# Strassen FFN on one Trainium2 core: the last phase's tile arithmetic on VectorE, and S3·T3 ahead of S4·B22

## The chip, the cores and the metric

One core of one Trainium2 chip runs the whole program in one launch. The metric is the device time of one execution in microseconds. The profile shows TensorE (PE, with its weight loads as PEld), VectorE (DVE), ScalarE (ACT), GpSimd (POOL) and the queue of SyncE (SP), which issues most of the DMAs.

## The reference, cut to what matters

The program is two transformer-like blocks in a row; the change touches only the last part of the second, its feed-forward network:

```
h = rms_norm_2(x, pre2_w) * (1 + sc2) + sh2
gate, up = split(h @ ffn_w_in, 2)           # 1024 tokens x 1024 -> 2 x 2816
y = (silu(gate) * up) @ ffn_w_out           # 1024 x 2816 -> 1024 x 1024
x = x + (1 + gt2) * rms_norm_2(y, post2_w)
```

Everything is fp32.

## The kernel before, in words

Activations lie with their features on the 128 partitions and the 1024 tokens along the free axis, in halves of H = 512. Each fp32 operand is split into a high part, which ACT copies (`hi`, `ah`, `tv`), and a low part, which DVE forms as source minus high (`lo`, `al`, `tv`). `mm3` multiplies such a pair by three matmuls (high·high, high·low, low·high). So every operand tile costs one ACT copy and one DVE subtraction before PE can use it.

The last phase, `phase_f`, does the following in order.

- The out projection, and `mid(0)` and `mid(1)` beside it: norm, residual, second norm, and the activation operands of the first FFN product, in two token halves. `mid(1)` makes T1, T2, B22, T3 and T4 in this order, four tiles of 128x512 each. T3 and T4 are differences of tiles `res`, by `psub`.
- The first FFN product (L1825 `variant`, L2091 `rest`). It is done as one level of Strassen-Winograd in 11 groups of the hidden dimension, with the weight variants A0, A1, S1, S2, S4, S3 and A22 in each group. Per group the variant code forms S1 (`padd`), S2, S4 and S3 (`psub`) for two weight blocks, eight operations of 128x512. Groups 0 to 3 first do A0 and A1, then the rest. The results go to DRAM as `ffa` (DMAs on POOL's queue).
- The second FFN product (the loop from L2277), 8 products n = 0 to 7 in the order of the tables `WV` and `XV`: A11·B11, S1·T1, S2·T2, S4·B22, S3·T3, A12·B21, and A22·T4 in two halves of 256 tokens. Each runs over KH = 11 blocks k with four PSUM banks. `fetch` loads activation tiles `c` from `ffa`, 7 steps of k ahead of the matmuls, into 8 buffers (SP queue). `parts` forms T1, T2, T3 and T4 by `psub` and splits them, 5 steps ahead, into 6 buffers `ah` and `al`. `variant2` loads weight blocks (`quad`, 128x2x512, from `wfo`, also on SP's queue) and forms S1, S2 and S4 in the tiles `sc`, and S3 from two fresh loads. `drain` adds a product's four PSUM banks into the output sums `yu`, `yz`, `yw`, `yx`.
- `finish`: norm of the result, residual, output. The token sums go over PE (transposes, L2480), so they stand in PE's order. Half of the residual additions are on POOL (L2230) except in the last piece.

`psub` and `padd` (L1859, L1856) are GpSimd's `tensor_tensor`; `psplit` is the split with its subtraction on GpSimd. It is used for T4 in the second product and for four variants of group 0. `add`, `sub` and `tt` (L2439) and `stt` (L2451) are DVE's; `act` (L2465) is ACT's.

PE's instructions run in the order in which the program writes them. For the other engines and the DMA queues a scheduler fixes the order when the program is built, from its own idea of when each operand will be there. Every engine then runs its instructions strictly in that fixed order. Generators such as `mid`, `drain` and `finish` are advanced by `tick` while the matmuls are written, which places their transposes in PE's order.

Of the kernel before, what the change touches and what calls it, by code (L numbers as in the profile page):

```python
# [8 lines left out]
F32 = mybir.dt.float32  # L9
F32R = mybir.dt.float32r  # L10
U32 = mybir.dt.uint32
AF = mybir.ActivationFunctionType
ALU = mybir.AluOpType
# [3 lines left out]
P = 128  # L17
T = 1024
H = 512
# [1745 lines left out]
class PhaseF:  # L1765

    WV = ["A11", "S1", "S2", "S4", "S3", "A12", "A22", "A22"]
    XV = [("B11", 0, H), ("T1", 0, H), ("T2", 0, H), ("B22", 0, H), ("T3", 0, H), ("B21", 0, H), ("T4", 0, 256), ("T4", 256, H)]  # L1770
    KH = 11


# [49 lines left out]
    def variant(self, n, g, v):  # L1823

        if n == 0:  # L1825
            self.fetch_raws(-1)
        hi = self.ring.tile([P, 1024], F32R, tag="hi", name=self.name("hi"))
        lo = self.ring.tile([P, 1024], F32R, tag="lo", name=self.name("lo"))
        if v[0] == "A" and len(v) == 2:
            self.split(hi, lo, self.raws["g", 2 * g + int(v[1])])  # L1830
        else:
            if v == "S1":
                self.sl[g] = self.base.tile([P, T], F32, tag="rmask", name=self.name("sl"))
            for i in range(2):
                c = slice(i * H, i * H + H)
                j = 2 * g + i
                up, s = self.raws["u", j], self.sl[g][:, c]
                gate = self.raws.get(("g", j))
                if v == "S1":
                    self.padd(s, up[:, :H], up[:, H:])  # L1840
                elif v == "S2":
                    self.psub(s, s, gate[:, :H])
                elif v == "S4":
                    self.psub(s, gate[:, H:], s)
                elif v == "S3":
                    s = self.fl.tile([P, H], F32, tag="s3", name=self.name("s3"), bufs=1)
                    self.psub(s, gate[:, :H], up[:, :H])
                else:
                    s = up[:, H:]
                (self.psplit if g < 1 and v != "A22" else self.split)(hi[:, c], lo[:, c], s)  # L1850
        self.fetch_raws(n)
        return hi, lo


    def padd(self, out, a, b):
        self.nc.gpsimd.tensor_tensor(out=out, in0=a, in1=b, op=ALU.add)  # L1856

    def psub(self, out, a, b):
        self.nc.gpsimd.tensor_tensor(out=out, in0=a, in1=b, op=ALU.subtract)  # L1859

    def psplit(self, hi, lo, src):

        self.act(hi, src, AF.Copy)
        self.psub(lo, src, hi.bitcast(F32))

    def quad(self, i, j, e, tag=None):

# [8 lines left out]
    def variant2(self, v, e):  # L1876
        n = (2 if e < 5 else 1) * H
        if v == "S1":
            s = self.sc[e] = self.sp.tile([P, n], F32, tag=f"sc{e}", name=f"sc{e}")
            a, b = self.quad(1, 0, e), self.quad(1, 1, e, "ru")  # L1880
            self.add(s, a, b)
        elif v in ("S2", "S4"):
            s, a = self.sc[e], self.quad(0, v == "S4", e)
            if v == "S2":
                self.sub(s, s, a)
            else:
                self.sub(s, a, s)
        elif v == "S3":
            s, b = self.quad(0, 0, e), self.quad(1, 0, e, "ru")
            self.sub(s, s, b)  # L1890
        else:
            s = self.quad(int(v[1]) - 1, int(v[2]) - 1, e)
        hi = self.ring.tile([P, 1024], F32R, tag="hi", name=self.name("hi"))
        lo = self.ring.tile([P, 1024], F32R, tag="lo", name=self.name("lo"))
        self.split(hi[:, :n], lo[:, :n], s)
        return hi, lo

    def phase_f(self, x):
        nc, tc = self.nc, self.tc
# [15 lines left out]
        y = self.resid()  # L1915
# [23 lines left out]
        def mid(half):  # L1939
# [74 lines left out]
                yield from wait(2)  # L2014
            for k in range(4):
                t = y[k][:, hs]
                self.psub(t, y[k + 4][:, hs], t)
                tags = (("acc0", "acc1"), ("acc0b", "acc1b"), ("rb0", "rb1"))
                self.split(*put("T3", *(tile2(tags[k]) if k < 3 else tile1(0))), t)
                yield from wait(2)  # L2020
            for k in range(4):
                t = y[k + 4][:, h0]
                self.psub(t, y[k][:, h0], t)
                self.split(*put("T4", *tile1(1 + k)), t)
                yield from wait(2)

# [95 lines left out]
        items = [(n, k) for n in range(8) for k in range(self.KH)]  # L2122
        made, fetched, tch = {}, {}, {}
        cnt = [0, 0]
        FETCH, AHEAD = 7, 5

        def fetch(upto):
            while cnt[0] < min(upto, len(items)):
                n, k = items[cnt[0]]
                cnt[0] += 1  # L2130
                v, t0, t1 = self.XV[n]
                k1, k2 = k, k + self.KH
                src = {"B11": [(k1, 0)], "B21": [(k2, 0)], "T1": [(k1, H), (k1, 0)], "T2": [(k2, H)], "B22": [(k2, H)],
                       "T3": [(k2, H), (k1, H)], "T4": []}[v]
                fetched[n, k] = ts = []
                for row, o in src:
                    ts.append(fl.tile([P, H], F32, tag="c", name=self.name("c"), bufs=8)[:, : t1 - t0])
                    nc.sync.dma_start(ts[-1], self.ad[row][:, o + t0 : o + t1])

        def parts(upto, dst=None):  # L2140
            while cnt[1] < min(upto, len(items)):
                n, k = items[cnt[1]]
                cnt[1] += 1
                v, t0, t1 = self.XV[n]
                f = fetched.pop((n, k))
                t = f[0] if f else tch[k][:, t0:t1]
                if v == "T1":
                    t = tch[k] = self.sp.tile([P, H], F32, name=f"tch{k}")
                    self.psub(t, f[0], f[1])
                elif v == "T2":  # L2150
                    t = tch[k]
                    self.psub(t, f[0], t)
                elif v == "T3":
                    self.psub(t, f[0], f[1])
                elif v == "B21":
                    self.psub(tch[k], tch[k], t)
                d = dst
                if d is None:
                    d = [self.sp.tile([P, H], F32R, tag=q, name=self.name(q), bufs=AHEAD + 1)[:, : t1 - t0] for q in ("ah", "al")]
                made[n, k] = d  # L2160
                (self.psplit if v == "T4" else self.split)(*d, t)

        def early_parts():
            fetch(3)
            t = [fl.tile([P, T], F32R, tag="ru", name=self.name("ae"), bufs=2) for _ in range(2)]
            t.append(self.hpool.tile([P, T], F32R, tag="h6", name=self.name("ae")))
            for k in range(3):
                parts(k + 1, (t[k][:, :H], t[k][:, H:]))

        for g in range(self.LEAD):  # L2170
# [24 lines left out]
        yv = {}  # L2195
# [12 lines left out]
        def finish(t0, t1):  # L2208
            n = t1 - t0
            half, o = t0 // H, t0 % H  # L2210
            hr = slice(t0 // P, t1 // P)
            rb = tp.tile([P, H], F32, tag="rb", name=self.name("rb"))[:, :n]
            xs = []
            for m in range(8):
                if m % 2 == 0:
                    t = tp.tile([P, 1024], F32, tag=f"sc{m // 2}", name=self.name("X"))
                xs.append(t[:, m % 2 * H : m % 2 * H + n])
                nc.sync.dma_start(xs[m], self.x3d[m][:, t0:t1])
            tail = t1 == H
            if not tail:  # L2220
                yield
            if t1 == 256:
                yield
            r = []
            yield from self.rstd_rows(accs[half][:, o : o + n], rt[:, hr], rtmp[:, hr], None if tail else rb, 1, r)
            rb = r[0] if tail else rb
            for m in range(8):
                t = yv[m, half][:, o : o + n]
                self.stt(t, t, c3[:, m : m + 1], rb, ALU.mult, ALU.mult)
                (nc.gpsimd if t1 < T and m % 2 else nc.vector).tensor_tensor(out=t, in0=t, in1=xs[m], op=ALU.add)  # L2230
                nc.sync.dma_start(self.out[m][:, t0:t1], t)
                if t1 == T and m % 2:
                    yield

        def drain(n, pss):

            for m, ps in enumerate(pss):
# [13 lines left out]
                    self.add(u, ps, u)  # L2251
                    self.add(w, ps, w)
                elif n == 3:
                    x = yv[m, 1] = tp.tile([P, H], F32, name=f"yx{m}")
                    self.add(x, ps, yv[m + 4, 1])
                    square(1, x)
                elif n == 4:
                    w = yv[m + 4, 1]
                    self.add(w, ps, w)
                    square(1, w)  # L2260
                    self.add(u, ps, u)
                elif n == 5:
                    self.add(z, ps, z)
                    square(0, z)
# [329 lines left out]
```

## Time and profile before

| | |
|---|---|
| runs, device time | 2215.13, 2215.93, 2217.55 us; median 2215.93 |
| the profiled execution, own time | 2213.25 us |
| its span (first to last instruction of the core) | 2211.4 us |
| PE busy | 2138.3 us, 97% of the span |
| DVE busy | 1511.8 us, 68% |
| ACT busy | 900.2 us, 41% |
| POOL busy | 394.7 us, 18% |

Times in the rows below count from the span's start. The profiled execution's own time is 1.85 us longer than its span, and 2.68 us below the median of the runs. The out projection ends and the first FFN product starts at about 1500 us; the second product begins at 1952 us, and its last matmul ends at 2194 us. A row of a timeline gives the start, the length of one instruction or of several of one kind in a row, and in brackets the idle time before it with the instruction that ended it.

### The profile page before, as it was taken

The page shows a single profiled execution, that of the slowest core. Times are in us where ns is not written, and L with a number is a line of the kernel's source. Part 1 is how long each engine was busy: PE and PEld are TensorE (multiplying, and loading weights), DVE is VectorE, ACT ScalarE, POOL GpSimd, SP SyncE. Part 2 cuts the span into 40 slices and gives each one's busy share as a digit, 9 for nine tenths or more (in the row PEclk, how much of TensorE's full clock was granted, in tenths as well). Part 3 has the DMA queues.
Part 4 walks back from the last instruction along what each step waited for, and adds up shares of the span by engine and source line. Part 5 has one row for each costly group of instructions (what it writes and reads, how often), then busy time and mean ns, then how long its engine had stood idle before and what let it go on. Part 6 is the DMA issues. An engine that isn't in the chain of part 4 may idle for free.

```text
span 2211.4 us, 29459 instructions
## 1 busy us (share of the span) xinstructions
PE 2138.3 (97%) x10998; PEld 1766.7 (80%) x10998; DVE 1511.8 (68%) x2160; ACT 900.2 (41%) x1522; POOL 394.7 (18%) x388
## 2 busy tenths in 40 slices
PE   8999999999999999999999999999799999999896
PEld 7988888887898898787887778877588888887676
DVE  7675687676595533759665347769958767669697
ACT  5553553443255553434262122445423323334243
POOL 1000000001111200000000000013644434325245
PEclk9999999999999999999999999999899999999998
DMA  5011106320553343265565176644143222377744
GB/s 176 30 41 45 47 29 214 100 86 29 188 170 110 109 135 129 94 202 180 159 205 162 69 241 190 210 162 136 60 138 115 86 86 72 108 249 251 243 164 160
DMA packets 149815, 297.59 MB, mean 135 GB/s; under 512 B 21520, under 2 KB 43936, under 8 KB 149416
## 3 DMA queue, kind: packets, MB, share of 16 engines
q1 hardware_dynamic: 135128, 271.33, 37.9%
q0 software_dynamic: 8128, 20.07, 2.6%
q10 hardware_dynamic: 6416, 4.31, 0.7%
q8 instruction: 87, 1.43, 0.3%
q14 instruction: 56, 0.46, 0.1%
HBM read 232.55 MB, written 61.90 MB: 133 GB/s over the span
## 4 chain that ended last, share of the span: by engine, by line
PE 73%; DVE 11%; issue 6%; DMA 5%; ACT 3%; POOL 2%; SPq 0%; POOLq 0%; DVEq 0%; ACTq 0%
PE mm L2471 55%; PE sm L2471 17%; DVE lo L2439 2%; DVE al L2439 2%; PE sm L2480 1%; DVE sc L2439 1%; POOL res L1859 1%; ACT hi L2465 1%; DVE acc L2439 1%; DMA ru<-in_wfi 1%; DVE rl L2451 1%; DMA adar<-in_adaw 1%; DMA mD<-mlrows 1%; DVE B L2451 0%; POOL lo L1859 0%
## 5 line engine op out<-in xcount | busy, mean ns | idle before, releaser
L2471 PE MATMUL mm<-rh,hi 128*128 128x512 f32 x1552 | 623.5, 402 | 0.6 <-DVE c L2439 0.4
L2471 PE MATMUL mm<-rh,lo 128*128 128x512 f32 x1552 | 605.7, 390 | 0.0
L2471 PE MATMUL mm<-rl,hi 128*128 128x512 f32 x1552 | 605.1, 390 | 0.2 <-DVE rl L2439 0.2
L2471 PEld LDWEIGHTS mm<-rh,hi 128*128 128x128 f32 x1552 | 291.4, 188 | 70.6 <-issue 9.1
L2471 PEld LDWEIGHTS mm<-rh,lo 128*128 128x128 f32 x1552 | 291.4, 188 | 62.5
L2471 PEld LDWEIGHTS mm<-rl,hi 128*128 128x128 f32 x1552 | 291.9, 188 | 59.8 <-issue 3.1
L2465 ACT ACTIVATE hi<-raw 128x1024 fp32r<-128x1024 f32 (+2 forms) x189 | 182.6, 970 | 363.9 <-PE mm L2471 265.1
L2439 DVE TENSOR_TENSOR lo<-raw,hi 128x1024 fp32r<-128x1024 f32 (+2 forms) x189 | 221.1, 1173 | 107.0 <-ACT hi L2465 105.4
L2471 PE MATMUL mm<-yr,hi 128*128 128x512 f32 x384 | 119.2, 390 | 1.3 <-ACT yr L2465 0.8
L2471 PE MATMUL mm<-tv,hi 128*128 128x512 f32 x312 | 102.0, 407 | 14.5 <-DVE tv L2439 7.1
L2471 PE MATMUL mm<-hi,rh 128*128 128x256 f32 (+1 forms) x384 | 110.7, 288 | 0.0
L2471 PE MATMUL mm<-hi,rl 128*128 128x256 f32 (+1 forms) x384 | 109.2, 284 | 0.0
L2471 PE MATMUL mm<-lo,rh 128*128 128x256 f32 (+1 forms) x384 | 109.2, 284 | 0.0
L1856 POOL TENSOR_TENSOR sl<-ru 128x512 f32<-128x512 f32 x22 | 37.9, 1722 | 307.3 <-DMA ru<-in_wfi 307.3
L2451 DVE SCALAR_TENSOR_TENSOR adaa<-adar,cact,adaa 128x512 f32<-128x512 f32 x84 | 62.9, 749 | 37.0 <-DMA adar<-in_adaw 36.1
L2471 PEld LDWEIGHTS mm<-yr,hi 128*128 128x128 f32 x384 | 72.1, 188 | 17.7 <-DVE yr L2451 1.6
L2471 PEld LDWEIGHTS mm<-tv,hi 128*128 128x128 f32 x312 | 60.8, 196 | 31.4 <-DVE tv L2439 9.4
L2465 ACT ACTIVATE hi<-sl 128x512 fp32r<-128x512 f32 x66 | 39.3, 626 | 110.1 <-PE sm L2471 64.1
L2554 POOL TENSOR_TENSOR hss<-hss,mhalf 128x4 f32<-128x4 f32 x16 | 16.2, 1015 | 361.8 <-DVE hss L2457 361.8
L2471 PEld LDWEIGHTS mm<-hi,rh 128*128 128x128 f32 x384 | 73.4, 191 | 1.7 <-issue 1.2
L2471 PE MATMUL mm<-yr,lo 128*128 128x512 f32 x192 | 74.7, 389 | 0.0
L2471 PEld LDWEIGHTS mm<-hi,rl 128*128 128x128 f32 x384 | 73.4, 191 | 0.7 <-issue 0.2
(526 smaller groups left out, 4255.3 us busy)
## 6 DMA issues: line engine op xcount, KB each, us to landing
raw<-in_w SPq DMA_DIRECT2D x60, 512.0 KB
adar<-in_adaw SPq DMA_DIRECT2D x96, 256.0 KB
c<-ffa SPq DMA_DIRECT2D x88, 256.0 KB
raw<-in_wfo SPq DMA_DIRECT2D x40, 512.0 KB
raw<-in_wfi SPq DMA_DIRECT2D x30, 512.0 KB
raw<-in_wo SPq DMA_DIRECT2D x24, 512.0 KB
ru<-in_wfi SPq DMA_DIRECT2D x22, 512.0 KB
raw<-in_wpj SPq DMA_DIRECT2D x32, 256.0 KB
```

Source lines behind the costliest of these rows:

```text
L1856: self.nc.gpsimd.tensor_tensor(out=out, in0=a, in1=b, op=ALU.add)
L1859: self.nc.gpsimd.tensor_tensor(out=out, in0=a, in1=b, op=ALU.subtract)
L2439: self.nc.vector.tensor_tensor(out=out, in0=a, in1=b, op=op)
L2451: self.nc.vector.scalar_tensor_tensor(out=out, in0=a, scalar=s, in1=b, op0=op0, op1=op1)
L2465: self.nc.scalar.activation(out=out, in_=a, func=f, scale=scale, **kw)
L2471: self.nc.tensor.matmul(out, lhsT=l, rhs=r, start=start, stop=stop)
L2480: self.nc.tensor.transpose(out, a, self.ident[:n, :n])
L2554: self.nc.gpsimd.tensor_tensor(out=out, in0=tmp, in1=self.mhalf[:, : out.shape[1]], op=ALU.pow)
```

## The change

All `tensor_tensor` work of this phase on tiles moves from GpSimd to VectorE: `padd`, `psub` and `psplit` are gone, and `add`, `sub` and `split` stand in their place. The residual additions of `finish` are all VectorE's. In the second product S3·T3 becomes product n = 3 and S4·B22 n = 4. S3 is formed as A22 − S2 (one load) in place of A11 − A21 (two loads), and T3 as T2 − B11 (one reload of B11) in place of B22 − B12 (two loads). For k of 7 and above B11 is loaded straight into the tile `tch`, stays there, and is not loaded again for T1. `drain` follows the new order.

```diff
-    WV = ["A11", "S1", "S2", "S4", "S3", "A12", "A22", "A22"]
+    WV = ["A11", "S1", "S2", "S3", "S4", "A12", "A22", "A22"]
...
                 if v == "S1":
-                    self.padd(s, up[:, :H], up[:, H:])
+                    self.add(s, up[:, :H], up[:, H:])
                 elif v == "S2":
-                    self.psub(s, s, gate[:, :H])
+                    self.sub(s, s, gate[:, :H])
...
-                (self.psplit if g < 1 and v != "A22" else self.split)(hi[:, c], lo[:, c], s)
+                self.split(hi[:, c], lo[:, c], s)
...
         elif v == "S3":
-            s, b = self.quad(0, 0, e), self.quad(1, 0, e, "ru")
-            self.sub(s, s, b)
+            s = self.quad(1, 1, e)
+            self.sub(s, s, self.sc[e])
...
             for k in range(4):
                 t = y[k][:, hs]
-                self.psub(t, y[k + 4][:, hs], t)
+                self.sub(t, y[k + 4][:, hs], t)
...
-                src = {"B11": [(k1, 0)], "B21": [(k2, 0)], "T1": [(k1, H), (k1, 0)], "T2": [(k2, H)], "B22": [(k2, H)],
-                       "T3": [(k2, H), (k1, H)], "T4": []}[v]
+                src = {"B11": [(k1, 0)], "B21": [(k2, 0)], "T1": [(k1, H)] + [(k1, 0)] * (k < FETCH), "T2": [(k2, H)],
+                       "T3": [(k1, 0)], "B22": [(k2, H)], "T4": []}[v]
...
                 if v == "T1":
-                    t = tch[k] = self.sp.tile([P, H], F32, name=f"tch{k}")
-                    self.psub(t, f[0], f[1])
+                    if k < FETCH:
+                        tch[k] = self.sp.tile([P, H], F32, name=f"tch{k}")
+                    t = tch[k]
+                    self.sub(t, f[0], f[1] if k < FETCH else t)
...
                 elif v == "T3":
-                    self.psub(t, f[0], f[1])
+                    self.sub(t, tch[k], t)
...
-                (self.psplit if v == "T4" else self.split)(*d, t)
+                self.split(*d, t)
...
                 elif n == 3:
-                    x = yv[m, 1] = tp.tile([P, H], F32, name=f"yx{m}")
-                    self.add(x, ps, yv[m + 4, 1])
+                    w = yv[m, 1] = yv[m + 4, 1]
+                    x = yv[m + 4, 1] = tp.tile([P, H], F32, name=f"yx{m}")
+                    self.add(x, ps, w)
+                    self.add(u, ps, u)
                     square(1, x)
                 elif n == 4:
-                    w = yv[m + 4, 1]
+                    w = yv[m, 1]
                     self.add(w, ps, w)
                     square(1, w)
-                    self.add(u, ps, u)
```

As built, POOL has 208 rows in place of 384, DVE 2279 in place of 2100, SP's queue 805 in place of 826 (loads of `c` from `ffa` 69 in place of 88, straight into `tch` 4 in place of none, loads of `ru` from `wfo` 6 in place of 12).

Three places show how the order moves. The first is DVE's order around the making of T3 and T4 in `mid(1)`, up to the first addition (`w<-mm_13679`) that frees a PSUM bank of the first product's S1 and S2. Before, behind the split of B22 (`rl`):

```order
L2439 TENSOR_TENSOR rl_12780<-res_12444,rh_12772 128x512
L2439 TENSOR_TENSOR tv_13733<-res_12440,tv_13732 128x512
L2439 TENSOR_TENSOR tv_13744<-res_12441,tv_13743 128x512
...
L2439 TENSOR_TENSOR tv_13791<-res_12444,tv_13791 128x512
L2439 TENSOR_TENSOR lo_13773<-sl_13774,hi_13772 128x512
L2439 TENSOR_TENSOR tv_13801<-res_12445,tv_13801 128x512
L2439 TENSOR_TENSOR tv_13816<-res_12446,tv_13816 128x512
L2439 TENSOR_TENSOR w_13723<-mm_13679,c_13214 128x512
```

and in the change:

```order
L2437 TENSOR_TENSOR rl_12780<-res_12444,rh_12772 128x512
L2437 TENSOR_TENSOR res_12440<-res_12444,res_12440 128x512
L2437 TENSOR_TENSOR res_12441<-res_12445,res_12441 128x512
...
L2437 TENSOR_TENSOR sl_13774<-ru_13719 128x512
L2437 TENSOR_TENSOR tv_13759<-res_12442,tv_13758 128x512
L2437 TENSOR_TENSOR sl_13774<-ru_13721 128x512
...
L2437 TENSOR_TENSOR res_12444<-res_12440,res_12444 128x512
...
L2437 TENSOR_TENSOR res_12447<-res_12443,res_12447 128x512
L2437 TENSOR_TENSOR w_13723<-mm_13679,c_13214 128x512
```

The subtractions that form T3 and T4 (`res<-res,res`) and the next variant (`sl<-ru`) now stand in DVE's own line, ahead of `w`.

The second place is DVE's order at the start of the second product, where `al_16546` is the low part of B11 for k = 3. Before:

```order
L2439 TENSOR_TENSOR lo_16519<-raw_16516,hi_16518 128x1024
L2439 TENSOR_TENSOR al_16546<-c_16537,ah_16545 128x512
```

and in the change:

```order
L2437 TENSOR_TENSOR lo_16519<-raw_16516,hi_16518 128x1024
L2437 TENSOR_TENSOR tch_16703<-c_16649,c_16651 128x512
L2437 TENSOR_TENSOR tch_16735<-c_16679,c_16681 128x512
L2437 TENSOR_TENSOR al_16546<-c_16537,ah_16545 128x512
```

T1's subtractions for k = 0 and 1, which belong to the next product, now stand ahead of it, and the four loads of `c` that they read stand on SP's queue ahead of the loads of B11 for k = 7 to 10.

The third place is SP's queue where S3's weights are loaded. Before, in the product S4·B22 (`c_17488<-ffa_13184` is the second operand of T3 for k = 0):

```order
L1873 DMA raw_17607<-in_wfo 128x2x512
L1873 DMA ru_17609<-in_wfo 128x2x512
L2138 DMA c_17466<-ffa_13205 128x512
L2138 DMA c_17486<-ffa_13195 128x512
L1873 DMA ru_17639<-in_wfo 128x2x512
L1873 DMA ru_17697<-in_wfo 128x2x512
L2218 DMA X_18061<-x3d_12454 128x512
L2138 DMA c_17488<-ffa_13184 128x512
L2218 DMA X_18061<-x3d_12455 128x512
L2218 DMA X_18064<-x3d_12456 128x512
L2138 DMA c_17515<-ffa_13196 128x512
L2138 DMA c_17517<-ffa_13185 128x512
```

and in the change, at the end of S2·T2:

```order
L1863 DMA raw_17192<-in_wfo 128x2x512
L2133 DMA c_17199<-ffa_13205 128x512
L2133 DMA c_17220<-ffa_13184 128x512
L1863 DMA raw_17239<-in_wfo 128x2x512
L2133 DMA c_17246<-ffa_13185 128x512
L2133 DMA c_17265<-ffa_13186 128x512
L1863 DMA raw_17284<-in_wfo 128x2x512
L2133 DMA c_17291<-ffa_13187 128x512
```

Each weight block of S3 is now one load with two activation loads behind it, no `ru` and no `X` between.

## Rows read from the trace of the kernel before

**Rows 1.** The page's busy times in us; the number behind x counts instructions.

```profile
PE 2138.3 (97%) x10998; PEld 1766.7 (80%) x10998; DVE 1511.8 (68%) x2160; ACT 900.2 (41%) x1522; POOL 394.7 (18%) x388
```

**Rows 2.** PE's waits from 1300 us on: total us, times, longest.

```profile
PE mm L2471 <- DVE al L2439: 12.5, 5, 8.7
PE mm L2480 <- DVE acc L2439: 10.8, 3, 4.6
PE mm L2471 <- DVE tv L2439: 7.1, 3, 3.6
PE mm L2471 <- DVE w L2439: 4.0, 1, 4.0
```

**Rows 3.** Windows: us, then PE, PEld, DVE, ACT, POOL busy, PEclk, DMA share, GB/s.

```profile
1541.00:1592.00 51.00, 35.81 (x117) 25.73 (x118) 49.10 (x50) 24.49 (x42) 35.65 (x21) 0.78 0.21 67
1610.00:1950.00 340.00, 339.59 (x1497) 280.40 (x1496) 241.12 (x316) 100.85 (x158) 133.43 (x109) 1.00 0.30 100
1952.00:1982.00 30.00, 30.00 (x134) 24.86 (x133) 18.74 (x19) 11.03 (x17) 9.87 (x7) 1.00 0.91 306
1982.00:2012.70 30.70, 30.33 (x134) 24.52 (x133) 28.36 (x21) 13.56 (x23) 21.02 (x12) 1.00 0.77 262
2012.70:2047.30 34.60, 31.29 (x134) 24.43 (x133) 33.53 (x34) 15.46 (x22) 10.03 (x5) 1.00 0.77 260
...
2078.20:2120.90 42.70, 33.25 (x134) 26.60 (x133) 31.15 (x29) 15.73 (x24) 23.18 (x15) 0.88 0.65 213
2120.90:2159.00 38.10, 34.32 (x140) 27.66 (x139) 34.80 (x42) 13.49 (x22) 13.39 (x10) 0.91 0.44 152
...
2174.90:2194.10 19.20, 16.76 (x138) 16.39 (x136) 15.57 (x26) 7.49 (x16) 12.98 (x14) 1.00 0.27 90
```

**Rows 4.** Timelines of DVE and POOL in `mid(1)`.

```profile
1544.12 2.44 DVE L2451 SCALAR_TENSOR_TENSOR res<-res,c,rb 128x512 f32<-128x512 f32 x2 [1.04 <-ACT rb L2465]
1562.85 1.75 DVE L2439 TENSOR_TENSOR tv<-res,tv 128x512 fp32r<-128x512 f32 x1
1589.61 0.68 DVE L2439 TENSOR_TENSOR w<-mm,c 128x512 f32<-128x512 f32 x1
...
1560.67 8.43 POOL L1859 TENSOR_TENSOR res<-res,res 128x512 f32<-128x512 f32 x5 [0.63 <-DVE res L2439]
```

**Rows 5.** Timeline of DVE at the start of the second product, POOL idle.

```profile
1954.81 3.09 DVE L2439 TENSOR_TENSOR al<-c,ah 128x512 fp32r<-128x512 f32 x5
```

**Rows 6.** Group by form, DVE, 1610 to 1950 us: busy, mean ns, idle before.

```profile
L2451 DVE SCALAR_TENSOR_TENSOR c<-c,c 128x512 f32<-128x512 f32 x18 | 22.9, 1271 | 0.3
```

**Rows 7.** Timelines at n = 0: SP, ACT, PE, POOL.

```profile
1953.79 0.34 SPq L2138 DMA_DIRECT2D c<-ffa  x1
1958.02 0.32 SPq L2138 DMA_DIRECT2D c<-ffa  x1
1960.78 1.08 SPq L2138 DMA_DIRECT2D c<-ffa  x1
...
1957.42 0.64 ACT L2465 ACTIVATE ah<-c 128x512 fp32r<-128x512 f32 x1 [1.64 <-DMA c<-ffa]
...
1960.53 0.39 PE L2471 MATMUL mm<-al,hi 128*128 128x512 f32 x1
...
1969.32 1.35 POOL L1859 TENSOR_TENSOR tch<-c,c 128x512 f32<-128x512 f32 x1 [14.72 <-DMA c<-ffa]
```

**Rows 8.** Timelines at n = 4: SP, DVE.

```profile
2075.87 8.60 SPq L2138 DMA_DIRECT2D c<-ffa  x5
2084.53 0.43 SPq L1873 DMA_DIRECT2D raw<-in_wfo  x1
...
2088.76 1.23 DVE L2439 TENSOR_TENSOR raw<-raw,ru 128x1024 f32<-128x1024 f32 x1 [14.96 <-issue]
```

**Rows 9.** Timeline of PE at n = 5.

```profile
2140.63 1.12 PE L2480 MATMUL mm<-ident,acc 128*128 128x128 f32 x4 [3.78 <-DVE acc L2439]
```

**Rows 10.** POOL's waits, 1952 to 2160 us.

```profile
POOL tch L1859 <- DMA c<-ffa: 37.6, 14, 14.7
```

More of the change, by code (lines that the diff above doesn't have):

```diff
@@ L1765 @@
 class PhaseF:
-    WV = ["A11", "S1", "S2", "S4", "S3", "A12", "A22", "A22"]
-    XV = [("B11", 0, H), ("T1", 0, H), ("T2", 0, H), ("B22", 0, H), ("T3", 0, H), ("B21", 0, H), ("T4", 0, 256), ("T4", 256, H)]
+    WV = ["A11", "S1", "S2", "S3", "S4", "A12", "A22", "A22"]
+    XV = [("B11", 0, H), ("T1", 0, H), ("T2", 0, H), ("T3", 0, H), ("B22", 0, H), ("B21", 0, H), ("T4", 0, 256), ("T4", 256, H)]
     KH = 11
@@ L1839, in variant @@
                 if v == "S1":
-                    self.padd(s, up[:, :H], up[:, H:])
+                    self.add(s, up[:, :H], up[:, H:])
                 elif v == "S2":
-                    self.psub(s, s, gate[:, :H])
+                    self.sub(s, s, gate[:, :H])
                 elif v == "S4":
-                    self.psub(s, gate[:, H:], s)
+                    self.sub(s, gate[:, H:], s)
                 elif v == "S3":
                     s = self.fl.tile([P, H], F32, tag="s3", name=self.name("s3"), bufs=1)
-                    self.psub(s, gate[:, :H], up[:, :H])
+                    self.sub(s, gate[:, :H], up[:, :H])
                 else:
                     s = up[:, H:]
-                (self.psplit if g < 1 and v != "A22" else self.split)(hi[:, c], lo[:, c], s)
+                self.split(hi[:, c], lo[:, c], s)
         self.fetch_raws(n)
         return hi, lo
[L1855 to L1864, printed above, removed]
     def quad(self, i, j, e, tag=None):
@@ L2022, in mid @@
                 t = y[k + 4][:, h0]
-                self.psub(t, y[k][:, h0], t)
+                self.sub(t, y[k][:, h0], t)
                 self.split(*put("T4", *tile1(1 + k)), t)
@@ L2124, in phase_f @@
         cnt = [0, 0]
-        FETCH, AHEAD = 7, 5
+        FETCH, AHEAD, EARLY = 7, 5, 3
         def fetch(upto):
@@ L2132, in fetch @@
                 k1, k2 = k, k + self.KH
-                src = {"B11": [(k1, 0)], "B21": [(k2, 0)], "T1": [(k1, H), (k1, 0)], "T2": [(k2, H)], "B22": [(k2, H)],
-                       "T3": [(k2, H), (k1, H)], "T4": []}[v]
+                src = {"B11": [(k1, 0)], "B21": [(k2, 0)], "T1": [(k1, H)] + [(k1, 0)] * (k < FETCH), "T2": [(k2, H)],
+                       "T3": [(k1, 0)], "B22": [(k2, H)], "T4": []}[v]
                 fetched[n, k] = ts = []
                 for row, o in src:
-                    ts.append(fl.tile([P, H], F32, tag="c", name=self.name("c"), bufs=8)[:, : t1 - t0])
+                    if v == "B11" and k >= FETCH:
+                        ts.append(self.sp.tile([P, H], F32, name=f"tch{k}"))
+                        tch[k] = ts[-1]
+                    else:
+                        ts.append(fl.tile([P, H], F32, tag="c", name=self.name("c"), bufs=8)[:, : t1 - t0])
                     nc.sync.dma_start(ts[-1], self.ad[row][:, o + t0 : o + t1])
@@ L2147, in parts @@
                 if v == "T1":
-                    t = tch[k] = self.sp.tile([P, H], F32, name=f"tch{k}")
-                    self.psub(t, f[0], f[1])
+                    if k < FETCH:
+                        tch[k] = self.sp.tile([P, H], F32, name=f"tch{k}")
+                    t = tch[k]
+                    self.sub(t, f[0], f[1] if k < FETCH else t)
                 elif v == "T2":
                     t = tch[k]
-                    self.psub(t, f[0], t)
+                    self.sub(t, f[0], t)
                 elif v == "T3":
-                    self.psub(t, f[0], f[1])
+                    self.sub(t, tch[k], t)
                 elif v == "B21":
-                    self.psub(tch[k], tch[k], t)
+                    self.sub(tch[k], tch[k], t)
                 d = dst
@@ L2160, in parts @@
                 made[n, k] = d
-                (self.psplit if v == "T4" else self.split)(*d, t)
+                self.split(*d, t)
         def early_parts():
-            fetch(3)
+            fetch(EARLY)
             t = [fl.tile([P, T], F32R, tag="ru", name=self.name("ae"), bufs=2) for _ in range(2)]
             t.append(self.hpool.tile([P, T], F32R, tag="h6", name=self.name("ae")))
-            for k in range(3):
+            for k in range(EARLY):
                 parts(k + 1, (t[k][:, :H], t[k][:, H:]))
@@ L2229, in finish @@
                 self.stt(t, t, c3[:, m : m + 1], rb, ALU.mult, ALU.mult)
-                (nc.gpsimd if t1 < T and m % 2 else nc.vector).tensor_tensor(out=t, in0=t, in1=xs[m], op=ALU.add)
+                self.add(t, t, xs[m])
                 nc.sync.dma_start(self.out[m][:, t0:t1], t)
```

## The prediction

> **What bounds the kernel now.** I read the page's busy times first: PE is busy in 97% of the span and DVE in 68% [rows 1]. So only the few per cent in which PE is kept waiting can be won, and what matters is where they lie. PE's waits from the last phase on name the releaser: DVE ends nearly all of them, with low parts of operands (`al`, `tv`), an addition that frees a PSUM bank (`w`) and the sum of squares (`acc`) [rows 2]. The windows by stage then show where. An undisturbed product of the second FFN stage takes 30 us: in the window of n = 0 PE is busy without a gap [rows 3]. Against that n = 1 takes 30.7, n = 2 34.6, n = 4 42.7, n = 5 38.1, and the last half product 19.2 for 15, which is 30.3 us lost together. Earlier, in `mid(1)`, PE is busy for 35.8 of 51 us at a granted clock of 0.78, while DVE is busy for 49.1 [rows 3]. From 1610 to 1950 us PE loses nothing (339.6 of 340).
>
> What makes DVE late? A `tv` subtraction takes 1.75 us in the timeline while POOL runs `res<-res,res`; an addition with one operand in PSUM, and subtractions while POOL is idle, take 0.68, or 0.62 each in a row of five [rows 4, 5]. POOL itself needs 8.43 us for five, 1.69 each [rows 4]. I conclude that a POOL operation on tiles makes a DVE operation with two SBUF inputs beside it take about twice as long. Groups in the first FFN product show it as a mean: 1.27 us for `c<-c,c` [rows 6].
>
> **First FFN product, 1610 to 1950 us.** The change adds 8 operations a group, so 72 in these nine groups: 72 x 0.62 = 45 us on DVE. Its busy time of 241 becomes at most 286 of 340 us, 84%, and less where stretched ones shorten (18 x (1.27 - 0.68) = 11 us in the one group of [rows 6]). DVE has the room, PE waits for nothing there. The variants now stand in DVE's line, so an addition behind one that waits for its weights waits too; PSUM banks cover that. POOL's queue keeps the stores to `ffa` and loses what stood ahead of them. Cost 0, bounds -3 to +1.
>
> **`mid(1)`.** From the first `res<-res,c,rb` to the end of `w<-mm,c` the old order has 45 DVE instructions and took 1590.3 - 1544.1 = 46.2 us [rows 4], 1.03 each. The new order has 60 there, as POOL's eight subtractions for T3 and T4 and several weight variants join. At 0.62, 37.2 us, plus some 1.5 us of waits for ACT as the row's 1.04 shows, that is 38.7. So `w`, for which PE waited 4.0 us [rows 2], comes 7.5 us sooner. Bounds: 3 if each costs 0.69 and the waits double, 14 if all of PE's idle 15 us but one go. I take **7.5 us gained**. POOL cannot be late any more; the next late thing would be ACT, busy for 24.5 of 51.
>
> **The start of the second product.** Here the order works against the change. `al` for k = 3, which PE uses at 1960.53, now stands behind T1's subtractions for k = 0 and 1. Those need four loads, of which the last will be issued where the fourth `c` load stood, at 1958.02. Two rows price a landing: the load issued at 1953.79 was used at 1957.42 (3.6 us), the one at 1960.78 at 1969.32 (8.5 us) [rows 7]. DMA is 0.91 busy here [rows 3]. So it lands at 1961.6 to 1966.5, and with two subtractions of 0.68 `al` is there at 1963.0 to 1967.9: PE loses 2.4 to 7.4 us. I take the near end, as that row is of the same few microseconds: **3 us lost** (0 to 9: 0 if the scheduler's waits fall otherwise, 9 with a slow clock after).
>
> **Products 1 to 3.** At 0.62 and 1.23 us for the 1024-wide ones [rows 8], DVE's work is 22 narrow and 11 wide operations per product and the drains: 27 us for n = 1, 30 for n = 2 (4 additions more), 32 for n = 3 (8 more), against 30 for PE. That is about what it does now with POOL's help (28.4 and 33.5 busy, [rows 3]), since its own ones are stretched today. With operands made five steps ahead the 2 us too many in n = 3 are covered. The 15 fewer loads of `c` (256 KB each) and 6 fewer weight loads (512 KB) relieve SP's queue and the DMA engines. I take +0.5 for n = 1 (of 0.7), +3.5 for n = 2 (0 to 4.6) and -0.5 for n = 3 (-3 to +1).
>
> **The stall in n = 4.** DVE idled for 14.96 us, because S3's weights were issued on SP's queue at 2084.53, behind five `c` loads that took 8.60 us to issue [rows 8]. They waited for `c` buffers, of which T3 took two for each k, freed by POOL's subtraction. In the new order each weight block stands ahead of two loads of one buffer each, with no second weight load and no `X` between. DVE needs the block for its own work five steps ahead, and nothing on SP's queue waits for POOL. I take 11.5 of the 12.7 lost us (8 to 12.7) as **gained**; S4·B22 behind it has single loads as before.
>
> **n = 5.** PE's token sums waited 3.78 us for `acc` [rows 9], and the clock fell to 0.91 in the window [rows 3]. DVE came into this product with work left from the late n = 4. Now the additions to `yu` are done one product earlier, and the 11 subtractions for B21 come to DVE: 11 + 11 narrow, 6 wide and the drain make 26 us of 30. I take **5.5 of 8.1 gained**, 0 to 7.
>
> **The rest.** In the half products T4's 22 low parts of 128x256 come to DVE: 22 x 0.34 (half of 0.68) = 7.5 us over 30 us, against stretches that go. Net 0, -5 to +3 (of the 4.2 lost now). The eight half additions of `finish`, no longer beside DVE's: 1 us lost, -1.5 to +1.
>
> **Sum.** 7.5 - 3 + 0.5 + 3.5 - 0.5 + 11.5 + 5.5 - 1 = 24 us. The profiled execution's own time is 2213.25, so 2189.3; the median of the runs shown is 2.7 above it, which gives **2192 us**. A difference of 0.2% (4.4 us) is about what a measurement of this kernel can tell from none. With the bounds added as independent errors (13 us towards slow, 8 towards fast) the forecast reaches from 2184 to 2205.
>
> **Rivals.**
>
> A. *The queue stall stays.* If the new single loads of T3 still hold SP's queue while the S3 block behind them is due, the part of the change on S3 does nothing: 2192 + 11.5 = 2203.5. For it: two `c` loads still stand between blocks, on eight buffers. Against: each buffer now serves a whole step. Chance 0.11.
>
> B. *Slower: DVE waits for loads in line.* POOL waited 37.6 us for `c` before T1's and T2's subtractions [rows 10], and nothing stood behind those waits but POOL's own work. On DVE, `al`, `lo` and drains stand behind each. The first, of 14.7, began before anything was due; the other 23 us and the upper bound at the start (7) make 30 us lost in n = 0 to 2, where I have a gain of 1. Then 2192 + 31 = 2223. It decides once these stalls take more than the 23 us won elsewhere. For it: DMA 0.91 and 0.77 busy [rows 3]. Against: loads run seven steps, 19 us, ahead, 15 of the loads of `c` are gone, and POOL's waits were partly for the buffers its own slowness held. Chance 0.11.
>
> C. *DVE is full, and POOL isn't what stretches it.* Then old operations keep their lengths and each added one costs 0.62: `mid(1)` 15 x 0.62 = 9.3 lost, n = 1 and 2 get 11 more (6.8) each on 28.4 and 33.5 busy us, so 35.2 and 40.3, which is 4.5 and 5.7 more than these products take now. With 3 lost at the start, 1 at the end, 11.5 still won and nothing in n = 5, that is 12 slower: 2228. Against: the same form of operation at 0.62 at 0.91 DMA share, with POOL idle [rows 3, 5]. Chance 0.03. The Trainium skill, "Perfetto Trace Analysis", section "Optimizing Scalar/DVE Operations", speaks for it: where DVE is saturated, moving work to GpSimd may make sense, and the change does the opposite where DVE is busy for 49 of 51 us. The same section adds that both share a read port of SBUF, so that it might not help; by the 1.75 us beside POOL the trace is with the second sentence.
>
> D. *Every stall goes*, upper bounds throughout: 14 + 0.7 + 4.6 + 12.7 + 7 + 3 = 42: 2174. Chance 0.05.
>
> The forecast keeps 0.70. The Trainium skill, "GPSIMD Engine Reference", section "Key points", calls DVE about twice as fast on elementwise work; the rows have 1.69 against 0.62. By the page's factor an added operation would be 0.85 (an estimate), and `mid(1)` would gain 4 instead of 7.5; the measured 0.62 decides.
>
> **How the numbers follow.** Slower by more than 0.2% are C and most of B: 0.03 + 0.07 = 0.10. Within it, the low part of B and the slow ends of A and the forecast: 0.05. Faster, the rest: 0.85. The range from 2176 to 2211 leaves out B, C, the slow end of A and the forecast (0.02) and most of D with the forecast's fast end (0.04), 0.20 together.
>
> **What would show it.** Right: no DVE operation of 128x512 over 0.7 us in `mid(1)`; `w<-mm,c` near 38 us behind the first `res<-res,c,rb`; a PE gap of 2 to 7 us in n = 0 ended by `al`; n = 4 and n = 5 within 32 us; DVE's idle time before S3's `raw` under 4 us. Wrong: PE gaps in n = 1 to 3 ended by `al` or `lo`, with DVE waiting for `c` (B); a gap of over 5 us in n = 3 or 4 with S3's `raw` late on SP (A); DVE operations that stay over 1 us without POOL (C).

## The result, and the profile after

The change takes 2177.2 us (median of 4 runs, 2174.98 to 2181.01) where the kernel before takes 2215.55 on the same chip: 0.983 of it, with a 95% interval of 0.981 to 0.984. The profiled execution took 2174.98 us with a span of 2173.3, which is 38.1 us less span than before. The forecast was 2192 with a range of 2176 to 2211. So faster was right and the time lies in the range, but only 1.2 us from its fast end: 24 us were forecast, 38 came.

The page's busy times after, against [rows 1]:

```profile
PE 2127.4 (98%) x10998; PEld 1763.7 (81%) x10998; DVE 1505.0 (69%) x2338; ACT 904.7 (42%) x1522; POOL 120.5 (6%) x210
```

DVE has 178 instructions more and is busy for 7 us less. POOL's 274 us are gone, and with them more DVE time than the added instructions cost.

The windows of the changed kernel by stage, in the columns of [rows 3]: `mid(1)`, the steady part of the first FFN product, the products n = 0 to 5, and the last half product:

```profile
1541.00:1592.00 51.00, 44.59 (x168) 34.00 (x167) 50.97 (x85) 26.84 (x47) 1.14 (x2) 0.90 0.21 67
1610.00:1940.00 330.00, 330.00 (x1458) 273.34 (x1457) 244.01 (x375) 100.63 (x157) 21.60 (x40) 1.00 0.29 99
1937.20:1971.90 34.70, 31.56 (x133) 25.71 (x133) 23.00 (x30) 14.22 (x22) 0.54 (x1) 0.95 0.97 337
1971.90:2001.90 30.00, 30.00 (x134) 24.85 (x133) 29.66 (x39) 14.84 (x24) 0.00 (x0) 1.00 0.87 293
2001.90:2031.80 29.90, 29.90 (x133) 24.78 (x132) 27.63 (x39) 12.22 (x17) 0.00 (x0) 1.00 0.39 133
2031.80:2061.70 29.90, 29.90 (x133) 24.76 (x133) 27.65 (x37) 12.86 (x18) 0.00 (x0) 1.00 0.75 240
2061.70:2091.60 29.90, 29.90 (x133) 24.76 (x133) 25.95 (x40) 14.49 (x21) 0.00 (x0) 1.00 0.60 209
2091.60:2123.30 31.70, 31.60 (x140) 25.52 (x139) 26.08 (x42) 13.40 (x22) 1.04 (x1) 1.00 0.45 148
...
2139.10:2155.80 16.70, 16.70 (x138) 16.49 (x137) 14.62 (x35) 6.80 (x16) 0.69 (x1) 1.00 0.20 69
```

In the same 51 us PE runs 168 matmuls where it ran 117 [rows 3]. The products n = 1 to 4 run without a gap. So does n = 5 but for 0.1 us: its 31.7 us hold 140 matmuls where n = 4 has 133. Only n = 0 has become longer. PE's waits from 1300 us on show the same, against [rows 2]:

```profile
PE mm L2478 <- DVE acc L2437: 4.5, 1, 4.5
PE mm L2469 <- DVE al L2437: 3.1, 1, 3.1
PE mm L2469 <- ACT tv L2463: 2.7, 3, 1.1
PE mm L2469 <- DVE c L2437: 2.3, 1, 2.3
...
PE mm L2469 <- DVE tv L2437: 1.4, 4, 0.5
```

The `al` wait is the one in n = 0; the 4.5 us for `acc` stand in the tail, behind the last matmul. The three `acc` waits of before had one of 4.6 there too.

Where the 38 us came from, read from the start of the first matmul of each stage in PE's timelines (a stage runs to the start of the next):

| stage | starts before, after | took before, after | gained | forecast |
|---|---|---|---|---|
| all up to n = 0 (`mid(1)` in it) | 0 | 1952.2, 1937.3 | 14.9 | 7.5 |
| n = 0 | 1952.15, 1937.25 | 29.9, 34.8 | -4.8 | -3 |
| n = 1 | 1982.07, 1972.00 | 30.8, 29.9 | 0.9 | 0.5 |
| n = 2 | 2012.86, 2001.92 | 34.6, 29.9 | 4.6 | 3.5 |
| n = 3 | 2047.42, 2031.84 | 30.9, 29.9 | 1.0 | -0.5 |
| n = 4 | 2078.31, 2061.76 | 42.7, 29.9 | 12.8 | 11.5 |
| n = 5 | 2121.05, 2091.68 | 38.0, 31.6 | 6.4 | 5.5 |
| n = 6 and 7 | 2159.08, 2123.32 | 34.8, 32.2 | 2.6 | 0 |
| tail (to the span's end) | 2193.91, 2155.56 | 17.5, 17.7 | -0.2 | -1 |

The first row is one pair of traces, and the start of the second product scatters. In eight traces whose kernels all have this part's arithmetic on VectorE (the change twice and six of the runs below) it lies between 1936.8 and 1941.0 us, so against 1952.2 the gain up to there is 11 to 15 us.

### The profile page after: what moved, and what is told of

Same layout as the page of the kernel before. It is cut to its first block, busy times and chain, and to the rows that moved or that the text cites. A ratio compares the mean times of both kernels' runs of the same rounds, so it can differ in the third digit from the quotient of the medians.

```text
span 2173.3 us, 29295 instructions
## 1 busy us (share of the span) xinstructions
PE 2127.4 (98%) x10998; PEld 1763.7 (81%) x10998; DVE 1505.0 (69%) x2338; ACT 904.7 (42%) x1522; POOL 120.5 (6%) x210
## 4 chain that ended last, share of the span: by engine, by line
PE 85%; DVE 8%; DMA 2%; issue 2%; ACT 2%; POOL 0%; SPq 0%; POOLq 0%; DVEq 0%; ACTq 0%
PE mm L2469 63%; PE sm L2469 21%; PE sm L2478 1%; DVE lo L2437 1%; DVE res L2437 1%; DVE res L2449 1%; DMA mD<-mlrows 1%; DVE rl L2449 0%; DVE B L2449 0%; ACT C L2463 0%; DVE rl L2437 0%; DVE tv L2437 0%; DVE acc L2437 0%; ACT T L2463 0%; ACT hi L2463 0%
## 5 line engine op out<-in xcount | busy, mean ns | idle before, releaser
L2469 PEld LDWEIGHTS mm<-rl,hi 128*128 128x128 f32 x1552 | 292.2, 188 | 59.4 <-issue 3.1
L2437 DVE TENSOR_TENSOR lo<-raw,hi 128x1024 fp32r<-128x1024 f32 (+2 forms) x189 | 209.9, 1113 | 94.2 <-ACT hi L2463 92.4
L2469 PEld LDWEIGHTS mm<-lo,rh 128*128 128x128 f32 x384 | 73.4, 191 | 0.0
L2469 PE MATMUL sm<-tv,hi 128*128 128x512 f32 x216 | 66.5, 389 | 0.0
```

Source lines behind the costliest of these rows:

```text
L2437: self.nc.vector.tensor_tensor(out=out, in0=a, in1=b, op=op)
L2469: self.nc.tensor.matmul(out, lhsT=l, rhs=r, start=start, stop=stop)
```

## The experiments

**The two parts apart.** The change has two parts: the arithmetic moves, and the order of products changes. The first kernel below does only the one, the second only the other. The edit of the first, on the kernel before (and the same for `psub`, `psplit` and the additions of `finish`):

```diff
-                    self.padd(s, up[:, :H], up[:, H:])
+                    self.add(s, up[:, :H], up[:, H:])
```

> The kernel before with its tile arithmetic on VectorE, but with its old order of products (S4 B22 as n = 3, S3 T3 as n = 4, S3 from two weight loads, T3 from two activation loads). Theory 1 (POOL's tile work stretches DVE's, and the reorder is what removes the stall in n = 4): the first FFN product ends about 14.9 us sooner as in the change, n = 0 loses nothing because al stands ahead of T1 here, n = 1, 2, 5 and 7 gain 0.9, 4.6, 6 and 2.6, but the gap of some 9 us in n = 4 stays, with S3's raw late on SP's queue: 2213 - 29 = about 2184. Rival (the stall in n = 4 came from POOL's slowness in freeing the c buffers, so moving the arithmetic is enough): n = 4 within 32 us, about 2172, below the change itself.

Measured: 2176.8 us (4 runs, 0.981 of the kernel before, 0.979 to 0.984), the time of the whole change. Its windows for n = 0, 3, 4 and 5:

```profile
1938.90:1968.80 29.90, 29.90 (x133) 24.76 (x132) 19.52 (x27) 11.13 (x17) 0.54 (x1) 1.00 0.88 297
2028.60:2058.50 29.90, 29.90 (x134) 24.75 (x133) 23.15 (x32) 12.23 (x17) 0.00 (x0) 1.00 0.89 297
2058.50:2088.40 29.90, 29.90 (x134) 24.75 (x133) 28.79 (x42) 13.77 (x21) 0.00 (x0) 1.00 0.74 248
2088.40:2123.70 35.30, 32.99 (x140) 26.68 (x139) 31.55 (x49) 13.49 (x22) 1.04 (x1) 0.95 0.48 157
```

The stall in n = 4 is gone with the old order and with its double loads. So moving the arithmetic is enough, as the rival said, and the new order, to which the forecast gave much of that term, isn't needed for it. The old order costs 3.6 us in n = 5 (35.3 for 31.7), where PE waits 2.3 us for `acc`, and saves 4.8 in n = 0.

The second kernel is the change with `psub`, `padd` and `psplit` put back.

> The change with GpSimd's arithmetic put back everywhere (variants, T3 and T4 in mid, T1, T2, T3 and B21, T4's low parts, half of the last additions); the new order of products, S3 from S2 and T3 from T2 stay. Theory 1: no gain up to the second product, DVE operations beside POOL at 1.1 to 1.8 us again, n = 2 and n = 5 still at 33 to 38, n = 4's or n = 3's gap of 9 us gone: 2213 - 12 = about 2201, 2196 to 2206. Rival (POOL holds the buffers): the gap for S3's weights stays in n = 3, 2208 to 2220.

Measured: 2202.1 us (4 runs, 0.992 of before, 0.991 to 0.994). Windows for n = 2 to 5:

```profile
2015.60:2055.60 40.00, 31.30 (x134) 24.41 (x133) 36.61 (x31) 13.97 (x20) 25.21 (x14) 1.00 0.48 158
2055.60:2085.50 29.90, 29.90 (x133) 24.75 (x133) 27.13 (x31) 11.78 (x17) 5.05 (x3) 1.00 0.62 207
2085.50:2115.40 29.90, 29.90 (x133) 24.75 (x133) 29.63 (x32) 13.64 (x21) 13.62 (x8) 1.00 0.73 245
2115.40:2148.10 32.70, 31.51 (x140) 25.41 (x139) 30.80 (x39) 13.50 (x22) 12.83 (x9) 1.00 0.49 163
```

The order alone removes the stall of n = 4 as well and most of n = 5's loss, and makes n = 2 worse (40.0 for 34.6, with four waits of PE for `al`, 8.7 us in all). It gains 16 us. The arithmetic alone gains 41 on that chip, and both together no more (39 there): the two parts remove the same stalls, so their gains don't add.

**What POOL does to DVE, measured by itself.** Two kernels add work on POOL to the change that nothing waits for:

```diff
+            if n == 1:
+                du = fl.tile([P, H], F32, tag="s3", name=self.name("du"), bufs=1)
+                self.act(du, tch[0], AF.Copy)
+                for _ in range(40):
+                    nc.gpsimd.tensor_tensor(out=du, in0=du, in1=du, op=ALU.subtract)
```

and in the second 80 times `nc.gpsimd.memset(du, 0.0)` in place of the subtractions.

> The change plus 40 subtractions of 128x512 on GpSimd on a tile of their own (du - du into du), from n = 1 on, for which nothing waits. Theory 1: DVE operations with two SBUF inputs beside them take 1.1 to 1.8 us in place of 0.68, over some 55 to 70 us; DVE, which is busy for 29.7 of 30 us in n = 1 now, falls behind, PE waits for al and lo, and the time rises by 8 to 25 us, with gaps in n = 1 to 3. Rival (it was the wait for POOL's results, or POOL's share of the line, that cost, not what runs beside): DVE stays at 0.68 and the time within 2 us of the change.

> The change plus 80 fills of the same 128x512 tile on GpSimd, which read nothing. If what stretches DVE is the reading of SBUF by both, DVE stays at 0.68 to 0.72 and the time within 3 us of the change; if any GpSimd work beside DVE stretches it, DVE's operations are at 1 us or more and the time rises as with the subtractions, in the proportion of the POOL time.

Measured: 2192.5 us with the subtractions, 2176.1 with the fills (one execution each). POOL is busy with them for 59.4 us (1.49 each) and 42.1 us (0.53 each). They began sooner than expected, in n = 0: the subtractions run from 1943 to 2006 us, the fills from 1945 to 1992. So groups of DVE by form are shown from 1960 to 1990 us, where POOL is at work throughout. With the subtractions beside:

```profile
L2442 DVE TENSOR_TENSOR al<-tch,ah 128x512 fp32r<-128x512 f32 x7 | 10.7, 1523 | 0.0
...
L2442 DVE TENSOR_TENSOR lo<-sc,hi 128x1024 fp32r<-128x1024 f32 x3 | 6.2, 2057 | 0.0
```

with the fills beside:

```profile
L2442 DVE TENSOR_TENSOR al<-tch,ah 128x512 fp32r<-128x512 f32 x11 | 7.6, 689 | 0.6 <-ACT ah L2468 0.5
L2442 DVE TENSOR_TENSOR lo<-sc,hi 128x1024 fp32r<-128x1024 f32 x5 | 6.1, 1223 | 2.0 <-ACT hi L2468 2.0
```

and in the change itself, with neither:

```profile
L2437 DVE TENSOR_TENSOR lo<-sc,hi 128x1024 fp32r<-128x1024 f32 x6 | 7.3, 1223 | 2.1 <-ACT hi L2463 2.1
L2437 DVE TENSOR_TENSOR al<-tch,ah 128x512 fp32r<-128x512 f32 x10 | 6.9, 687 | 0.3 <-ACT ah L2463 0.3
```

So no wait for a result of POOL is needed: POOL work that reads SBUF, beside DVE, costs 15 us (2192.5 against the change's 2177.8 on the same chip), and PE waits for `al` again: 4.7 us in n = 0 where the change has 3.1, and 6.7 us in n = 1 where it has none. Each operation takes about 0.83 us longer in both widths, so "twice" fits the 512-wide ones (2.2 times) and is too much for the 1024-wide (1.7 times). Fills of the same tile cost nothing.

An addition with its first operand in PSUM (`yw<-sm,yu`) wasn't beside POOL in these two runs. It was in the run with the order alone, where all four such additions of n = 2 keep their 0.68 us. Timelines of DVE and POOL there:

```profile
2032.30 1.75 DVE L2448 TENSOR_TENSOR al<-tch,ah 128x512 fp32r<-128x512 f32 x1
2033.97 0.68 DVE L2448 TENSOR_TENSOR yw<-sm,yu 128x512 f32<-128x512 f32 x1
...
2031.83 3.36 POOL L1860 TENSOR_TENSOR c<-tch,c 128x512 f32<-128x512 f32 x2 [0.54 <-DMA c<-ffa]
```

The Trainium skill, "SBUF — State Buffer", section "Who interferes with whom", states this rule: a DVE instruction with two SBUF inputs contends with a GpSimd instruction that reads SBUF, not with one that only writes, and one with at most one SBUF input, outside DVE's two-port modes, doesn't contend. The rows of these three runs agree with it.

**Which POOL work cost what.** Three kernels put one share of the arithmetic back on POOL in the changed kernel: the variants, T3's and T4's eight subtractions in `mid(1)`, or the 44 subtractions of the second product. The edit of the second:

```diff
-                self.sub(t, y[k + 4][:, hs], t)
+                self.psub(t, y[k + 4][:, hs], t)
...
-                self.sub(t, y[k][:, h0], t)
+                self.psub(t, y[k][:, h0], t)
```

> The change with the weight variants of the first FFN product (S1, S2, S4, S3 and the splits of group 0) back on GpSimd. If the variants' stretching makes the loss in mid(1), most of the 14.9 us of the first product go back: second product starts at 1945 to 1952 in place of 1937, time 2183 to 2190. If T3's and T4's eight subtractions make it, the start is within 3 us of 1937 and the time 2175 to 2179. From 1610 us on PE loses under 1 us either way.

> The change with T3's and T4's eight subtractions in mid(1) back on GpSimd. Eight times 1.7 us of POOL beside DVE stretch up to some 12 DVE operations by about 1.05 us, 12.6, against 8 x 0.6 = 4.8 us that leave DVE: the second product starts 3 to 8 us later, time 2178 to 2184. If the variants alone make the loss: within 2 us of the change, or 2 to 4 us faster as DVE has less to do.

> The change with the 44 subtractions for T1, T2, T3 and B21 in the second product back on GpSimd. As in the run with the order alone: n = 2 takes about 40 us in place of 30 with gaps ended by al, n = 0 loses nothing of its 4.8 (T1's subtractions are out of DVE's line), the others stay near 30: 2175 + 10 - 4 = 2178 to 2186. If the operations' stretch there is covered by the five steps ahead: 2169 to 2173, faster than the change.

Measured, one execution each: 2186.0, 2179.6 and 2184.0 us, on another chip, on which the kernel before took 2218.9 and the change wasn't run. The second product starts at 1948.4 with the variants on POOL and at 1941.1 with the eight subtractions, where the change has 1937.3. The first lies outside the scatter given above, the second just at its edge (the third kernel, with `mid(1)` as in the change, has 1941.0), so for the eight subtractions that start shows little. What doesn't scatter is the length of the piece in `mid(1)` that the forecast priced, from the first `res<-res,c,rb` to the end of `w<-mm,c`: 46.2 us before, 36.8 in all eight traces with the arithmetic on VectorE. Its two ends and the window in the columns of [rows 3], with the variants on POOL:

```profile
1544.14 2.45 DVE L2460 SCALAR_TENSOR_TENSOR res<-res,c,rb 128x512 f32<-128x512 f32 x2 [1.04 <-ACT rb L2474]
...
1586.55 0.68 DVE L2448 TENSOR_TENSOR w<-mm,c 128x512 f32<-128x512 f32 x1
...
1541.00:1592.00 51.00, 36.00 (x125) 26.44 (x126) 49.67 (x63) 25.46 (x44) 25.63 (x15) 0.87 0.25 78
```

and with the eight subtractions on POOL (`w` is the first of the two):

```profile
1541.40 1.40 DVE L2460 SCALAR_TENSOR_TENSOR res<-res,c,rb 128x512 f32<-128x512 f32 x2
...
1581.19 1.27 DVE L2448 TENSOR_TENSOR w<-mm,c 128x512 f32<-128x512 f32 x2
...
1541.00:1592.00 51.00, 40.93 (x152) 30.78 (x151) 50.98 (x72) 27.22 (x46) 14.27 (x9) 0.83 0.21 69
```

The piece takes 43.1 and 40.5 us, 6.3 and 3.7 more than in the change, so both shares count, the variants more. DVE is full in both and in the change; what differs is how many instructions it gets done (63, 72, and 85 in the change). The third kernel loses 9.6 us in n = 2 (39.5) and none of the 4.8 in n = 0, as expected: T1's subtractions had left DVE's line there.

**The stall in n = 4 of before.** One edit on the kernel before, T3's subtractions:

```diff
-                    self.psub(t, f[0], f[1])
+                    self.sub(t, f[0], f[1])
```

> The kernel before with one edit: T3's 11 subtractions in the second product are on VectorE, all other arithmetic and the order of products stay. Theory 2 (the stall in n = 4 was POOL's T3 subtractions, which held the c buffers and so SP's queue, not the number of loads): n = 3 and n = 4 take 30 to 32 us each, n = 5 comes without the backlog, 2213 - 14 to 20 = 2193 to 2200. Theory 1 (the double loads make it): a gap of 5 us or more in n = 4 with S3's raw late, 2206 to 2214.

Measured: 2210.6 us, one execution. Windows for n = 3, 4 and 5:

```profile
2048.50:2080.10 31.60, 30.52 (x133) 24.61 (x133) 23.68 (x32) 12.42 (x17) 0.00 (x0) 1.00 0.86 277
2080.10:2113.80 33.70, 31.26 (x133) 24.34 (x133) 29.21 (x35) 13.98 (x21) 9.52 (x6) 1.00 0.72 237
2113.80:2154.70 40.90, 33.90 (x140) 26.65 (x139) 38.55 (x45) 13.48 (x22) 17.10 (x12) 0.92 0.45 147
```

The stall in n = 4 shrinks to 3.8 us, so POOL's T3 subtractions were what made it long. But the time was a miss, 8 us under the 2218.9 of the kernel before on that chip, where 14 to 20 were expected: in n = 5 DVE is busy for 38.6 of 40.9 us, beside POOL's B21 subtractions, and PE waits for `acc`. The longest of these waits is the one in n = 5:

```profile
PE mm L2480 <- DVE acc L2439: 14.2, 3, 7.0
```

It was 3.78 us before [rows 9]. So of the 9 us that n = 4 gives back n = 5 loses 2.9 (40.9 against 38.0), where the expectation had it gain too. On SP's queue nine `c` loads still held the head for 10.60 us here, but DVE waited at most 1.8 us for S3's weights, against 14.96 in [rows 8]. Whether POOL's subtractions did harm by freeing the buffers late or by stretching DVE isn't separated by this run.

**The loss in n = 0, and versions without it.** The first kernel takes the kept B11 out of the change; the second keeps it and makes five operand tiles ahead instead of three (two more tiles from freed ones); the third adds to the first a later T3 and T4 in `mid(1)` (`wait(8)` ahead of T3, `wait(16)` ahead of T4).

```diff
-                "T1": [(k1, H)] + [(k1, 0)] * (k < FETCH)
+                "T1": [(k1, H), (k1, 0)]
...
-        FETCH, AHEAD, EARLY = 7, 5, 3
+        FETCH, AHEAD, EARLY = 7, 5, 5
...
+            yield from wait(8)
             for k in range(4):
                 t = y[k][:, hs]
```

> The change itself once more, on the chip of the next three, as their measure: 2174 to 2181.

> The change without the kept B11: B11 goes through the c buffers for every k and T1 is formed from two loads for every k, as before. In the order this puts the low parts of B11 for k = 3 to 6 ahead of T1's first subtractions again. Theory (n = 0 loses its 4.8 us because DVE stands in line before T1's subtractions, whose loads are late): no gap in n = 0, n = 1 to 7 as in the change, 2177 - 4.8 = about 2171 to 2173. Rival (n = 0 loses because the loads and DMA are late there in any case, whoever asks): a gap of 2 us or more ended by al stays in n = 0, 2175 to 2181.

> The change with five instead of three operand tiles of B11 made before the first product ends (EARLY = 5). T1's subtractions stay ahead of the next low part in DVE's line, but PE has 5.4 us more to work on while DVE waits 2.5 + 4.4 us. Same theory: the gap of 3.5 us in n = 0 goes, 2171 to 2174. Rival as there: it only moves to k = 5.

> The run without the kept B11, and T3 and T4 of mid(1) written 8 and 16 slots of 0.64 us later, which in DVE's order puts the two additions c<-mm, that free PSUM banks, ahead of T3's subtractions. If PE's gap of 2.7 us there was DVE's line, it goes, and the second product starts 2 to 5 us sooner: 2167 to 2170. If the later T3 and T4 only shift the wait to their own use: no gain on the run without the kept B11, within 2 us.

| | median, us (runs) | against before, with interval |
|---|---|---|
| the change again | 2177.8 (5) | 0.983, 0.982 to 0.985 |
| without the kept B11 | 2173.3 (4) | 0.981, 0.979 to 0.982 |
| five tiles ahead | 2173.0 (4) | 0.981, 0.979 to 0.982 |
| later T3 and T4 | 2178.8 (4) | 0.983, 0.982 to 0.985 |

The window of n = 0 in the first of them:

```profile
1940.10:1970.00 29.90, 29.90 (x133) 24.77 (x132) 19.86 (x27) 11.09 (x17) 0.54 (x1) 1.00 0.90 303
```

DMA is as busy as before (0.90 for 0.91 in [rows 3]), and n = 0 takes 29.9 us without a gap. With five tiles ahead DVE still waits for T1's loads, and PE doesn't feel it. DVE's timeline and the window of n = 0 there:

```profile
1944.19 0.69 DVE L2439 TENSOR_TENSOR tch<-c,c 128x512 f32<-128x512 f32 x1 [3.23 <-DMA c<-ffa]
...
1950.14 0.69 DVE L2439 TENSOR_TENSOR tch<-c,c 128x512 f32<-128x512 f32 x1 [4.05 <-DMA c<-ffa]
...
1937.60:1967.60 30.00, 30.00 (x133) 24.75 (x132) 17.80 (x24) 10.62 (x16) 0.54 (x1) 1.00 0.80 273
```

So the loss was the place of T1's subtractions in DVE's line, ahead of the low parts that PE needed, and not the late loads by themselves. Both are 4.5 to 4.8 us faster than the change by their medians on the same chip. All runs without the kept B11 (2172.7 to 2173.7) lie below all of the change's (2176.1 to 2184.4); those with five tiles ahead (2170.7 to 2176.9) overlap them a little. The later T3 and T4 are a miss. The two additions did move ahead, but PE then waited 10.6 us for `w` (one wait), which now ended behind T4's four subtractions and all but one of its low parts in DVE's line.

## Why the prediction was right, point by point

- *POOL beside DVE makes DVE's operations about twice as long*: right for 512-wide operations with two inputs in SBUF, and shown by the added POOL work. No `tv` subtraction in `mid(1)` takes over 0.7 us in the timeline of DVE now; 1.75 was in [rows 4]. The sign named every operation of that width, and `res<-res,c,rb` still takes 0.75 to 0.77.
- *First product, 1610 to 1950 us, cost 0*: right. PE is busy for 330.00 of 330 us, DVE for 244 (74%).
- *`mid(1)`, 7.5 us*: right in kind, mis-sized, and the largest error of the sum: 14.9 in this pair of traces (11 to 15 by the others), over the upper bound of 14. Timelines of DVE in the changed kernel, the two ends of the piece, and of PE behind it:

```profile
1541.16 1.43 DVE L2449 SCALAR_TENSOR_TENSOR res<-res,c,rb 128x512 f32<-128x512 f32 x2
...
1577.28 0.70 DVE L2437 TENSOR_TENSOR w<-mm,c 128x512 f32<-128x512 f32 x1
```

```profile
1578.12 0.70 PE L2469 MATMUL mm<-tv,hi 128*128 128x512 f32 x2 [0.92 <-ACT tv L2463]
```

  The piece takes 36.8 us, 1.9 less than the 38.7 forecast, so it is 9.4 us shorter and not 7.5. It also begins sooner here, 1541.16 for 1544.12, which the forecast left out. That start lies between 1539.3 and 1544.0 in the eight traces, so how much of it is due to the change isn't shown. PE's same matmul stood at 1590.43 before, so 12.3 us were won by then; the other 2.6 came behind it, where the granted clock was 0.84 from 1590.43 to 1600 us before and is 1.00 from 1578.12 to 1588 now.
- *n = 0, 3 us lost*: right in kind; 4.8, of which the gap is 3.1 and the rest the clock behind it (0.95 in the window). DVE waited 2.54 and 4.35 us for the two loads:

```profile
1942.54 0.69 DVE L2437 TENSOR_TENSOR tch<-c,c 128x512 f32<-128x512 f32 x1 [2.54 <-DMA c<-ffa]
1947.59 0.69 DVE L2437 TENSOR_TENSOR tch<-c,c 128x512 f32<-128x512 f32 x1 [4.35 <-DMA c<-ffa]
```

- *n = 1 to 3*: right within 1.5 us. DVE fills 29.7 of 30 us in n = 1 and PE still doesn't wait.
- *n = 4, 11.5 us*: right in size (12.8), but its reason wasn't told apart. The step credited the single loads of the new order together with SP's queue no longer waiting for POOL; the run with the arithmetic alone shows that the old order with its double loads doesn't stall either. Either part is enough, and that the size came out doesn't show the reason.
- *n = 5, 5.5 us*: 6.4, all that there was: the forecast took the loss against 30 us, but n = 5 without a gap takes 31.7. The new order is worth 3.6 of it by the run with the old one; that this is the additions done one product earlier fits PE's 2.3 us for `acc` there, but wasn't tested apart.
- *The half products, 0*: 2.6 came. In the last half product, which without a gap takes 16.7 us and not the 15 it was measured against, the stretches that go outweigh the low parts that arrive: DVE does 35 instructions in 14.62 busy us, where it did 26 in 15.57 [rows 3].
- Rival A didn't occur. B occurred in n = 0 alone: DVE waited 6.9 us in all for `c` before T1's or T2's subtractions, where POOL had waited 37.6 [rows 10]. C is excluded by the unstretched 0.69. D, all stalls gone, was nearest: 2174 against 2177, and 0.05 was too little for it. The bounds were taken as independent, but one cause, POOL reading beside DVE, lay under most of the terms, so they erred together to the fast side.

## What to carry to other kernels

Where DVE's two-input operations take about twice their usual time, look at whether GpSimd reads SBUF beside them; then GpSimd's help can cost more than it saves even where DVE is full, and moving it to DVE can make DVE's busy time shorter, as here. Before crediting a reorder, run it without the other part of the change: here both removed the same stalls. And when an instruction that waits for a load moves into a busy engine's line, look at what stands behind it: two subtractions early cost 4.8 us, which two more operand tiles made ahead give back.

## What was not expected of the hardware

The size of the effect: 40 POOL subtractions that nobody waits for, 59.4 us of POOL time, cost the kernel 15 us, while 80 fills of 42.1 us cost nothing that the runs show (2176.1 in the change's range of 2175 to 2184). And DVE's total: with 178 instructions more it is busy for 7 us less.
